# The bias of the forgetting attention as one piece for each query tile, its mask added by an accumulating DMA

## The chip, the cores and the metric

The kernel runs on one core of a Trainium2 chip. The metric is the device time of one execution in microseconds (us). The kernel before took 2027.2 us (median of three executions, 2025.74 to 2028.43).

TensorE (PE) multiplies matrices into PSUM, VectorE (DVE) and ScalarE (ACT) work on tiles in SBUF and PSUM, GpSimd (POOL) works on tiles in SBUF and issues accumulating DMAs, and SyncE (SP) issues plain DMAs. Each engine takes its instructions in a fixed order and stands still while the next one waits.

## The reference, cut to what matters

A block of three transformer layers on 512 tokens of width 1024. Its last two layers hold a forgetting attention (8 heads of 64) beside a retention branch. In one of these layers, for the attention alone:

```
log_f  = log_sigmoid(f_logit + b_forget)            # 512 x 8
c      = cumsum(log_f over tokens)                  # one row of 512 numbers per head
scores = (q_i @ k.T) * 64 ** -0.5                   # 128 queries of block i x 512 keys
bias   = c_i[:, None] - c[None, :]
logits = where(key <= query, scores + bias, -inf)
out_i  = softmax(logits) @ v
```

In a softmax over keys `c_i` drops out (it is the same along a row), so a head needs the row of `c` over the keys, the same for every query, and the causal mask, which matters only in the 128x128 square on the diagonal.

## The kernel before, in words

The 512 tokens are four tiles of 128. Each weight block of 512 KB is loaded by SyncE into one of three `wr` buffers, and split into a high and a low half in float32r: ScalarE writes `wh`, VectorE writes `wl` (`wblk`, line 351; six buffers of each). Every product is three matmuls (high by high, high by low, low by high).

`block2` (line 1261) is one of the two layers with the forgetting attention. It projects the values, then the forget gates, and writes the 8 rows of `c` to DRAM (`cd`). Then for each of four pairs of heads it projects q and k (two `proj_a` of 24 matmuls, each in one of four PSUM banks `mm`) and spawns a thread `attention_pair` (line 507). After the four pairs comes the projection of the retention values (`proj_b` with column 2568), which fills four `mm` banks at once.

`attention_pair` first makes its operands for the two heads: `qs`, `kh` and `kl` read the two `mm` banks on ScalarE and VectorE, so a bank is free again only after the second head's `qs` or `kl`. For each head it then takes the query tiles t = 3, 2, 1, 0: scores of 128(t+1) keys into an `at` bank, one or two reductions on VectorE that add the bias and keep the row's minimum (the scores carry a minus sign), an exponential on ScalarE, a reciprocal, and a scaling on VectorE. When all four tiles are done, TensorE transposes the probabilities, VectorE and ScalarE copy them out of PSUM, and TensorE multiplies with the values.

`fox_bias` (line 1193) gives the reductions their bias. Per head it loads the row of `c` into all 128 partitions (`row`, 256 KB), and GpSimd adds the constant `tri` (0 on and below the diagonal, 1e30 above it, repeated for each tile) into a second tile `cm`. Tile t then needs two reductions: the keys before the diagonal with `row`, the diagonal square with `cm` (tile 0 needs the second only). The bias of the first block's attention (`moba_bias`) is one piece for each tile already.

What sets the order: `Weave` (line 160) runs the threads against a model of each engine's cost (the classes `Weave` and `Engine`; DMAs are not in that model) and records TensorE's instructions in the order in which the model lets threads proceed. The order on the other engines is made by a scheduler when the program is built. `load` (line 345) places a plain DMA on SyncE's queue behind the newest weight load.

Of the kernel before, what the change touches and what calls it, by code (L numbers as in the profile page):

```python
# [14 lines left out]
ALU = mybir.AluOpType  # L15
# [4 lines left out]
P, T, D = 128, 512, 1024  # L20
# [133 lines left out]
class Event:  # L154


    t = None
# [110 lines left out]
def model_kernel(ctx: ExitStack, tc: tile.TileContext, I, out):  # L268
    nc = tc.nc
# [13 lines left out]
    act, dve, pool = Engine(nc.scalar, wv, 0.2, 0.83), Engine(nc.vector, wv, 0.17, 1.04), Engine(nc.gpsimd, wv, 0.25, 2.1)  # L283
    uid = [0]

    def nm(s):
        uid[0] += 1
        return f"{s}_{uid[0]}"

    def bt(s="b", dt=F32):  # L290
        return pb.tile([P, T], dt, tag="b", name=nm(s))
# [31 lines left out]
    def copy(o, i):  # L323
        act.activation(o, i, AF.Copy)
# [20 lines left out]
    def load(dst, src):  # L345

        with tc.issue_after(last_dma[0].ins):
            nc.sync.dma_start(dst, src)

    def wblk(*key, pieces=1):  # L350
        key = key if len(key) == 7 else (*key, "")
        off, size = offs[key]
        nk = (key[3] - key[2]) // P
        raw = pw.tile([P, 1024], F32, tag="wr", name=nm("wr"), bufs=3)
        src = I["wall"][off : off + size].rearrange("(p w) -> p w", p=P)
        hi = pw.tile([P, 1024], F32R, tag="wh", name=nm("wh"))
        cuts = [slice(1024 // pieces * i, 1024 // pieces * (i + 1)) for i in range(pieces)]
        for c in cuts:
            with tc.issue_after(xdma[0].ins) if xdma else nullcontext():
                last_dma[0] = nc.sync.dma_start(raw[:, c], src[:, c])  # L360
            copy(hi[:, c], raw[:, c])
        if key[6]:
            h3 = hi.rearrange("p (k w) -> p k w", k=nk)
            r3 = raw.rearrange("p (k w) -> p k w", k=nk)
            sub_lo(h3[:, :, 32:64], r3[:, :, 32:64], h3[:, :, 32:64])
            return h3
        lo = pw.tile([P, 1024], F32R, tag="wl", name=nm("wl"))
        for c in cuts:
            sub_lo(lo[:, c], raw[:, c], hi[:, c])
        return hi.rearrange("p (k w) -> p k w", k=nk), lo.rearrange("p (k w) -> p k w", k=nk)  # L370
# [48 lines left out]
    def proj_b(name, l, k0, k1, c, acts, done, koff=0, tail=0, wait_k=False, wait_t=False, pre=None):  # L419


        pss = [mm_ps() for _ in range(NT)]
        ks = list(range(k0 // P, k1 // P))
        steps = [ks[i : i + 2] for i in range(0, len(ks) - tail, 2)] + ([ks[len(ks) - tail :]] if tail else [])
        for st in steps:
            if pre is not None:
                pre(st[0])
            pieces = 2 if pre is not None and st[0] == 0 else 1
            ws = [wblk(name, l, k * P, (k + 2) * P, c, c + 512, pieces=pieces) for k in st[::2]]
            if pre is not None:  # L430
                pre(st[1])
            if wait_k:
                for k in st:
                    yield acts.ev[k - koff]
            for t in range(NT):
                if wait_t:
                    yield acts.ev[t]
                last = st[-1] == ks[-1]
                yield from form_b(pss[t], ws, acts, [k - koff for k in st], t, st[0] == ks[0], last)
                if last:  # L440
                    done(t, pss[t])


    def const_src(n):
        return I["c128"][:, slice(*_AT[n])]

    def const(n):
        src = const_src(n)
        t = bt(n)[:, 0 : src.shape[1]]
        load(t, src)  # L450
        return t
# [4 lines left out]
    def col(n, i=0):  # L456
        return cols[:, _COL[n][0] + i : _COL[n][0] + i + 1]
# [42 lines left out]
    def row_bcast(src, n0):  # L500

        t = bt("row")
        load(t, bass.AP(tensor=src.tensor, offset=src.offset + n0, ap=[[0, P], [1, T]]))
        return t
# [97 lines left out]
    def token_rows(src, t, n):  # L602
        return src[t * P : t * P + P, 512 * n : 512 * n + 512]
# [334 lines left out]
    def to_tokens(dst, scaled):  # L938
        def done(t, ps):
            v = bt("v")  # L940
            if scaled:
                act.activation(v, ps, AF.Identity, scale=r1[:, t : t + 1])
            else:
                copy(v, ps)
            dst.append(v)

        return done

    def low_proj(w, n, acts):

        ps = mm_ps()
        for k in range(8):
            mm(ps, w[:, k, :], acts.hs[k], k == 0, False)
            mm(ps, w[:, k, :], acts.ls[k], False, k == 7)
            yield 0
        f = bt("low")
        copy(f[0:n], ps[32 : 32 + n])
        dve.tensor_tensor(f[0:n], ps[0:n], f[0:n], ALU.add)
        return f
# [230 lines left out]
        yield from block2(0, xw2, h)  # L1190


    def fox_bias(cd, tri):
        def bias(h):
            cb, cm = row_bcast(cd, T * h), bt("cm")
            pool.tensor_tensor(cm, cb, tri, ALU.add)

            def pieces(t):
                d = (P * t, P * t + P, cm[:, P * t : P * t + P])
                return [d] if t == 0 else [(0, P * t, cb[:, 0 : P * t]), d]  # L1200

            return pieces

        return bias

# [55 lines left out]
    def block2(l, xw, h):  # L1261
        fv = []
        yield from proj_b("w_in_2", l, 0, D, 1024, xw, to_tokens(fv, False), tail=8, wait_t=True)
        f = yield from low_proj(wblk("w_in_2", l, 0, D, 1536, 1544, "low"), 8, xw)
        a = bt("fa")
        dve.tensor_scalar(f[0:8], f[0:8], col(f"bf{l}")[0:8], None, ALU.add)
        log_sigmoid(f[0:8], f[0:8], a[0:8])
        dve.tensor_tensor_scan(a[0:8], one[0:8].to_broadcast([8, T]), f[0:8], 0.0, ALU.mult, ALU.add)
        cd = pd.tile([8, T], F32, tag="cd", name=nm("cd"))
        nc.sync.dma_start(cd, a[0:8])  # L1270
        bias = fox_bias(cd, const("tri"))
        mix = Acts(8, "mix")
        for i in range(4):
            qk = []
            for j in range(2):
                qk.append((yield from proj_a("w_in_2", l, 512 * j + P * i, xw)))

            def operands(q, k):
                def get():
                    return q, k, -0.125, None  # L1280
                    yield

                return get

            wv.spawn(attention_pair(i, operands(*qk), fv, bias, mix), 1)
        vs = []
        yield from proj_b("w_in_2", l, 0, D, 2568, xw, to_tokens(vs, False))
        ccos, csin = const("cc"), const("ss")
        decay, xi, zeta = const("decay"), const("xi"), const("zeta")
        sgs = []  # L1290
        for i in range(4):
            qk = []
            for j in range(2):
                ps = yield from proj_a("w_in_2", l, 1544 + 512 * j + P * i, xw)
                a, b = bt("ra"), bt("rb")
                copy(b[0:64], ps[64:128])
                copy(b[64:128], ps[0:64])
                dve.tensor_tensor(a, ps, ccos, ALU.mult)
                pool.tensor_tensor(b, b, csin, ALU.mult)
                pool.tensor_tensor(a, a, b, ALU.add)  # L1300
                qk.append(a)
            sgs.append([Event(), bt("sg")])
            wv.spawn(ret_head(l, i, *qk, vs, decay, xi, zeta, sgs[i], mix), 1)
        for i in range(4):
            ps = yield from proj_a("w_in_2", l, 3080 + P * i, xw)
            ev, sg = sgs[i]
            sigmoid(sg, ps)
            dve.tensor_tensor(sg, ps, sg, ALU.mult)
            wv.mark(ev)
        hT = Acts(8, "hT", True)  # L1310
        ln1 = LayerNorm(h, norm_rows("ln1_g_2", "ln1_b_2", l))

        def norm1(t):
            ln1.apply(t)
            yield from to_features(h[t], hT, t)

        yield from out_proj("w_out_2", l, mix, h, ALPHA, ln1.part, norm1)
        ln2 = LayerNorm(h, norm_rows("ln2_g_2", "ln2_b_2", l))
        if l == 0:
            xw2 = Acts(8, "xT", True)  # L1320

        def norm2(t):
            ln2.apply(t)
            if l == 0:
                yield from to_features(h[t], xw2, t)
            else:
                for n in range(2):
                    nc.sync.dma_start(token_rows(out, t, n), h[t][n])

        yield from ffn("w_ff1_2", "w_ff2_2", l, hT, h, ALPHA, ln2.part, norm2, 6)  # L1330
        if l == 0:
            yield from block2(1, xw2, h)
# [45 lines left out]
```

## Time and profile before

| | |
|---|---|
| median of three executions | 2027.2 us |
| the profiled execution | 2023.48 us, its span 2021.7 us |
| TensorE busy | 1986.7 us, 98% of the span |
| VectorE busy | 1165.7 us, 58% |
| ScalarE busy | 936.4 us, 46% |
| GpSimd busy | 281.8 us, 14% |
| DMA | 240.50 MB, mean 119 GB/s |

How to read it: a group of instructions is named by line, engine, operation and tiles (output <- inputs, buffer numbers left out). Line 311 is every matmul, line 320 every transpose, line 262 every instruction on VectorE, ScalarE and GpSimd, line 348 every plain load other than weights. Of the tiles, `mm` and `at` are PSUM banks, `ea`, `eb`, `ec` the scores and probabilities of a head (tile 3 in `ea`, tile 2 and tile 0 in `eb`, tile 1 in `ec`), `mx` their small columns. The two layers with the forgetting attention have theirs at about 860 to 955 us and 1456 to 1552 us.

### The profile page before, as it was taken

The page shows a single profiled execution, that of the slowest core. Times are in us where ns is not written, and L with a number is a line of the kernel's source. Part 1 is how long each engine was busy: PE and PEld are TensorE (multiplying, and loading weights), DVE is VectorE, ACT ScalarE, POOL GpSimd, SP SyncE. Part 2 cuts the span into 40 slices and gives each one's busy share as a digit, 9 for nine tenths or more (in the row PEclk, how much of TensorE's full clock was granted, in tenths as well). Part 3 has the DMA queues.
Part 4 walks back from the last instruction along what each step waited for, and adds up shares of the span by engine and source line. Part 5 has one row for each costly group of instructions (what it writes and reads, how often), then busy time and mean ns, then how long its engine had stood idle before and what let it go on. Part 6 is the DMA issues. An engine that isn't in the chain of part 4 may idle for free.

```text
span 2021.7 us, 25560 instructions
## 1 busy us (share of the span) xinstructions
PE 1986.7 (98%) x9574; PEld 1646.3 (81%) x9574; DVE 1165.7 (58%) x2052; ACT 936.4 (46%) x1639; POOL 281.8 (14%) x313
## 2 busy tenths in 40 slices
PE   8999999999999999999999999999999999999998
PEld 7777788888888888877888888888877889888886
DVE  6676444444556573475455656665575565656655
ACT  6566354333545453365332554552464324545550
POOL 2000110000212110010401201110111401211101
PEclk9999999999999999999999999999999999999999
DMA  6422123242766543332233745552422234655551
GB/s 202 157 90 78 53 65 103 94 146 74 187 162 133 155 125 115 100 106 88 78 126 111 158 138 134 148 148 81 132 94 84 73 115 146 135 156 156 131 142 42
DMA packets 93483, 240.50 MB, mean 119 GB/s; under 512 B 10734, under 2 KB 11200, under 8 KB 93360
## 3 DMA queue, kind: packets, MB, share of 16 engines
q1 hardware_dynamic: 72624, 201.12, 29.6%
q0 software_dynamic: 20736, 37.76, 11.5%
q8 instruction: 75, 1.23, 0.2%
q14 instruction: 48, 0.39, 0.1%
HBM read 236.69 MB, written 4.77 MB: 119 GB/s over the span
## 4 chain that ended last, share of the span: by engine, by line
PE 95%; DVE 2%; ACT 2%; issue 0%; POOL 0%; DMA 0%; POOLq 0%; DVEq 0%; SPq 0%; ACTq 0%
PE mm L311 67%; PE at L311 26%; PE at L320 2%; ACT wh L262 0%; DVE wl L262 0%; ACT kh L262 0%; ACT qs L262 0%; DVE og L262 0%; DVE h L262 0%; DVE qs L262 0%; POOL mv L262 0%; POOL gm L262 0%; ACT kl L262 0%; DMA xr<-in_xT_dram 0%; DVE cum L262 0%
## 5 line engine op out<-in xcount | busy, mean ns | idle before, releaser
L262 DVE TENSOR_TENSOR wl<-wr,wh 128x1024 fp32r<-128x1024 f32 (+1 forms) x265 | 334.9, 1266 | 316.7 <-ACT wh L262 315.1
L262 ACT ACTIVATE wh<-wr 128x1024 fp32r<-128x1024 f32 (+1 forms) x268 | 283.1, 1057 | 486.0 <-PE mm L311 346.4
L262 DVE TENSOR_TENSOR wl<-sw,wh 128x512 fp32r<-128x512 f32 x252 | 167.2, 688 | 179.1 <-ACT wh L262 178.9
L262 ACT ACTIVATE wh<-sw 128x512 fp32r<-128x512 f32 x252 | 151.2, 626 | 229.5 <-PE at L311 124.0
L311 PE MATMUL at<-hTh,wl 128*128 128x512 f32 (+1 forms) x640 | 242.2, 378 | 0.0
L311 PE MATMUL at<-hTh,wh 128*128 128x512 f32 (+1 forms) x640 | 242.2, 378 | 0.0
L311 PE MATMUL at<-hTl,wh 128*128 128x512 f32 (+1 forms) x640 | 242.2, 378 | 0.0
L311 PE MATMUL mm<-xTh,wh 128*128 128x512 f32 x536 | 213.9, 399 | 0.0
L669 POOL DMA_DIRECT2D sw<-in_wall_dram x144 | 126.6, 1016 | 600.2 <-DVE wl L262 504.6
L311 PE MATMUL mm<-xTl,wh 128*128 128x512 f32 x536 | 209.0, 390 | 0.0
L311 PE MATMUL mm<-xTh,wl 128*128 128x512 f32 x512 | 200.0, 391 | 0.0
L311 PE MATMUL mm<-wh,xl 128*128 128x512 f32 x504 | 196.1, 389 | 0.0
L311 PE MATMUL mm<-wl,xh 128*128 128x512 f32 x504 | 196.1, 389 | 0.0
L311 PE MATMUL mm<-wh,xh 128*128 128x512 f32 x504 | 196.1, 389 | 0.0
L311 PE MATMUL mm<-wh,xTh 128*128 128x512 f32 x352 | 144.5, 411 | 12.8 <-ACT wh L262 6.6
L311 PE MATMUL mm<-wl,xTh 128*128 128x512 f32 x352 | 139.0, 395 | 0.0
L311 PE MATMUL mm<-wh,xTl 128*128 128x512 f32 x352 | 138.9, 395 | 0.0
L311 PEld LDWEIGHTS at<-hTh,wl 128*128 128x128 f32 x640 | 120.4, 188 | 22.5
L311 PEld LDWEIGHTS at<-hTl,wh 128*128 128x128 f32 x640 | 120.4, 188 | 22.4
L311 PEld LDWEIGHTS at<-hTh,wh 128*128 128x128 f32 x640 | 120.4, 188 | 22.4
L311 PEld LDWEIGHTS mm<-xTh,wh 128*128 128x128 f32 x536 | 100.8, 188 | 19.6 <-ACT wh L262 0.5
L311 PEld LDWEIGHTS mm<-xTl,wh 128*128 128x128 f32 x536 | 100.9, 188 | 18.7
(283 smaller groups left out, 3705.1 us busy)
## 6 DMA issues: line engine op xcount, KB each, us to landing
wr<-in_wall_dram SPq DMA_DIRECT2D x266, 512.0 KB, 3.6
sw<-in_wall_dram SPq DMA_DIRECT2D x144, 256.0 KB, 5.7
sw<-in_wall_dram POOLq DMA_DIRECT2D x144, 256.0 KB, 6.0
row<-cd SPq DMA_DIRECT2D x16, 256.0 KB, 4.1
revp<-rev SPq DMA_DIRECT2D x1, 2560.0 KB
xr<-in_xT_dram SPq DMA_DIRECT2D x8, 256.0 KB, 6.1
g<-revp SPq DMA_DIRECT2D x8, 256.0 KB, 4.1
h<-in_x_dram SPq DMA_DIRECT2D x8, 256.0 KB, 5.7
```

What stands on the lines that cost most here:

```text
L262: return f(out, *a, **k)
L311: nc.tensor.matmul(out, lhsT, rhs, start=start, stop=stop, skip_group_check=more)
L320: nc.tensor.transpose(out, in_, ident)
L669: nc.gpsimd.dma_start(t, src, accum_op=ALU.add)
```

## The change

Each query tile gets a bias tile of its own: for each head and each t, SyncE loads 128(t+1) entries of the row of `c` into all partitions (`c1`, `c2`, `c3` hold tiles 1; 2 and 0; 3), and an accumulating DMA on GpSimd's queue adds the 128x128 mask from DRAM to the last 128 columns. GpSimd's addition, the constant tile `tri` and its load are gone, and every tile has one reduction.

```diff
-    def fox_bias(cd, tri):
+    def fox_bias(cd):
+        room = [None]
         def bias(h):
-            cb, cm = row_bcast(cd, T * h), bt("cm")
-            pool.tensor_tensor(cm, cb, tri, ALU.add)
-
-            def pieces(t):
-                d = (P * t, P * t + P, cm[:, P * t : P * t + P])
-                return [d] if t == 0 else [(0, P * t, cb[:, 0 : P * t]), d]
-
-            return pieces
+            if h % 2 == 0:
+                room[0] = bt("c1")
+            a, b, c = bt("c3"), bt("c2"), room[0]
+            h0 = 256 * (h % 2)
+            tiles = [b[:, 384:512], c[:, h0 : h0 + 256], b[:, 0:384], a]
+            for t in (3, 2, 1, 0):
+                n = P * t + P
+                load(tiles[t], bass.AP(tensor=cd.tensor, offset=cd.offset + T * h, ap=[[0, P], [1, n]]))
+                nc.gpsimd.dma_start(tiles[t][:, P * t : n], const_src("tri")[:, 0:P], accum_op=ALU.add)
+            return lambda t: [(0, P * t + P, tiles[t])]
...
-        bias = fox_bias(cd, const("tri"))
+        bias = fox_bias(cd)
```

The new form moves instructions on every engine, in the same way in both layers. The first place is SyncE's queue at the first pair of heads, where `wr` is a weight block and `row` or `c` the bias; before:

```order
L1270 DMA cd_6799<-fa_6792 8x512 [waits DVE_49]
L360 DMA wr_7458<-in_wall_dram 128x1024 [waits DMAHW3_49,DVE_49]
L348 DMA row_6900<-cd_6799 128x512 [waits DMAHW7_49,PE_49]
L360 DMA wr_7575<-in_wall_dram 128x1024 [waits DMAHW4_49,DVE_49]
L348 DMA row_6913<-cd_6799 128x512 [waits PE_49]
```

and now:

```order
L1276 DMA cd_6799<-fa_6792 8x512 [waits DVE_49]
L360 DMA wr_7577<-in_wall_dram 128x1024 [waits DMAHW3_49,DVE_49]
L348 DMA c_1264_6899<-cd_6799 128x512 [waits DMAHW6_49,PE_49]
L348 DMA c_1265_6900<-cd_6799 128x384 [waits PE_49]
L348 DMA c_1263_6898<-cd_6799 128x256 [waits DMASW1_49,PE_49]
L348 DMA c_1265_6900<-cd_6799 128x128
L348 DMA c_1263_6898<-cd_6799 128x256 [waits DMAHW4_49]
L348 DMA c_1269_6918<-cd_6799 128x512 [waits DMAHW5_49,PE_49]
L348 DMA c_1270_6919<-cd_6799 128x384 [waits DMASW2_49]
L348 DMA c_1270_6919<-cd_6799 128x128 [waits DMAHW7_49]
L360 DMA wr_7656<-in_wall_dram 128x1024 [waits DMAHW0_49,DVE_49]
```

Eight loads for two heads stand in a row, and the next weight load behind them. GpSimd issues the eight masks in the same order of tiles.

The second place is TensorE from the last matmul of the fourth pair's k projection (`mm_7250` before, `mm_7358` now) to the first matmul of the retention values that wants the bank of the fourth pair's q. Before (rows that repeat are left out):

```order
L311 MATMUL mm_7250<-xTh_3889,wl_7255 128x512
L311 MATMUL mm_7364<-wh_7369,xTh_3888 128x512
...
L320 MATMUL at_7377<-ident,eb_7066 128x128 [waits DVE_49,PE_49]
...
L311 MATMUL mm_7365<-wh_7369,xTh_3888 128x512
...
L320 MATMUL at_7419<-ident,ec_7063 128x128 [waits DVE_49,PE_49]
...
L311 MATMUL mm_7366<-wh_7369,xTh_3888 128x512 [waits DVE_49]
```

and now:

```order
L311 MATMUL mm_7358<-xTh_3889,wl_7363 128x512
L311 MATMUL mm_7438<-wh_7443,xTh_3888 128x512
...
L311 MATMUL at_7451<-pta_7274,v_6687 64x512 [waits Activation_49]
...
L311 MATMUL at_7462<-kh_7297,qs_7296 128x512 [waits DVE_49]
...
L320 MATMUL at_7541<-ident,eb_7318 128x128 [waits DVE_49]
...
L311 MATMUL mm_7439<-wh_7443,xTh_3888 128x512
...
L311 MATMUL mm_7440<-wh_7443,xTh_3888 128x512 [waits DVE_49]
```

Before, 12 matmuls of the projections and 8 transposes stand between the two; now 12 matmuls, the second pair's product with the values (`at_7451`), the eight score matmuls of the third pair's second head (from `at_7462`) and 4 transposes.

The third place is VectorE at the same point, up to the second `qs` of the fourth pair, which frees that bank. Before:

```order
L262 TENSOR_TENSOR wl_7840<-wr_7836,wh_7837 128x1024 [waits DMAHW0_49,PE_49,Activation_49]
L262 RECIPROCAL mx_7340<-mx_7340 128x1 [waits Activation_49]
L262 COPY pta_7326<-at_7377 128x512 [waits PE_49]
L262 TENSOR_SCALAR eb_7194<-eb_7194,mx_7340 128x384 [waits DVE_49]
L262 SCALAR_TENSOR_TENSOR qs_7383<-mm_7155,qs_7383 64x512 [waits Activation_49]
L262 TENSOR_TENSOR kl_7385<-mm_7250,kh_7384 64x512 [waits Activation_49]
L262 SCALAR_TENSOR_TENSOR qs_7396<-mm_7155,qs_7396 64x512 [waits Activation_49]
```

and now:

```order
L262 TENSOR_TENSOR wl_7866<-wr_7862,wh_7863 128x1024 [waits DMAHW3_49,PE_49,Activation_49]
L262 TENSOR_TENSOR mixl_6810<-at_7451,mixh_6802 128x512 [waits Activation_49]
L262 ISA ea_7433,mx_7465<-at_7462,c_1360_7305 128x512 [waits DMAHW2_49,DMASW5_49,PE_49]
...
L262 ISA eb_7434,mx_7488<-at_7478,c_1361_7306 128x128 [waits DMASW7_49]
...
L262 SCALAR_TENSOR_TENSOR qs_7495<-mm_7249,qs_7495 64x512 [waits Activation_49]
...
L262 TENSOR_SCALAR ea_7433<-ea_7433,mx_7465 128x512 [waits DVE_49]
...
L262 TENSOR_SCALAR eb_7434<-eb_7434,mx_7488 128x128 [waits DVE_49]
L262 TENSOR_TENSOR kl_7497<-mm_7358,kh_7496 64x512 [waits Activation_49]
L262 SCALAR_TENSOR_TENSOR qs_7515<-mm_7249,qs_7515 64x512 [waits Activation_49]
```

The fourth pair's two `qs` now stand behind the split of the product with the values (`mixl`) and behind a whole softmax of the head before: four reductions and four scalings.

## Rows read from the trace of the kernel before

**Rows 1.** Page, chain that ended last: shares of the span by engine

```profile
PE 95%; DVE 2%; ACT 2%; issue 0%; POOL 0%; DMA 0%; POOLq 0%; DVEq 0%; SPq 0%; ACTq 0%
```

**Rows 2.** TensorE's waits, whole trace: us in total, times, longest

```profile
PE mm L311 <- DVE qs L262: 5.9, 2, 2.9
...
PE at L311 <- ACT pta L262: 1.7, 2, 0.9
```

**Rows 3.** Chain, 860 to 1120 us: start us, us, what

```profile
902.20 3.87 PE mm L311 x17
...
906.09 1.07 ACT wh L262
...
907.18 1.22 DVE wl L262
...
910.14 0.69 DVE kl L262
...
910.86 0.63 ACT kl L262
...
911.50 0.60 ACT qs L262
...
912.12 0.70 DVE qs L262
```

**Rows 4.** Windows: us, busy by engine, PEclk, DMA share, GB/s

```profile
913.00:914.00 1.00, 1.00 (x6) 0.82 (x7) 0.97 (x2) 0.66 (x2) 0.73 (x1) 1.00 0.09 33
1509.00:1511.00 2.00, 2.00 (x7) 1.51 (x6) 1.48 (x3) 0.69 (x2) 2.00 (x2) 0.54 0.00 0
1511.00:1513.00 2.00, 2.00 (x9) 1.54 (x7) 0.00 (x0) 0.00 (x0) 0.41 (x1) 0.61 0.00 0
```

**Rows 5.** VectorE groups by form, 855 to 960 us: count | busy us, mean ns | idle

```profile
L262 DVE CUSTOM_DVE_ANT_0 ea<-at,row 128x384 f32<-128x384 f32 x8 | 4.4, 551 | 0.3 <-PE at L311 0.2
L262 DVE TENSOR_SCALAR ea<-ea,mx 128x512 f32<-128x512 f32 x8 | 3.9, 482 | 0.0
...
L262 DVE CUSTOM_DVE_ANT_0 ea<-at,cm,mx 128x128 f32<-128x128 f32 x8 | 2.7, 340 | 0.1
```

**Rows 6.** The same view, 180 to 300 us

```profile
L262 DVE CUSTOM_DVE_ANT_0 ea<-at,g 128x512 f32<-128x512 f32 x2 | 1.4, 686 | 0.6 <-PE at L311 0.6
```

**Rows 7.** Timeline of SyncE's queue, 845 to 965 us: start us, us, what

```profile
858.99 0.37 SPq L348 DMA_DIRECT2D row<-cd  x1
...
876.79 0.90 SPq L348 DMA_DIRECT2D row<-cd  x2
```

**Rows 8.** Timeline of GpSimd, 840 to 965 us

```profile
862.97 1.56 POOL L262 TENSOR_TENSOR cm<-row,tri 128x512 f32<-128x512 f32 x1 [129.75 <-DMA row<-cd]
```

**Rows 9.** Timeline of VectorE, 855 to 960 us

```profile
867.60 2.34 DVE L262 TENSOR_TENSOR wl<-wr,wh 128x1024 fp32r<-128x1024 f32 x1 [0.89 <-ACT wh L262]
```

**Rows 10.** Chain again: pieces of one kind of TensorE work

```profile
869.41 1.28 PE at L311 x8
...
878.16 0.44 PE at L320 x4
```

**Rows 11.** Timeline of TensorE, 897 to 902 us

```profile
897.71 1.08 PE L311 MATMUL at<-pta,v 128*64 128x512 f32 x4
...
900.01 0.44 PE L311 MATMUL at<-kh,qs 128*128 128x384 f32 x1
```

**Rows 12.** Line 669, accumulating loads: ns min/median/max; landing min/median/max

```profile
L669 POOL DMA_DIRECT2D sw<-in_wall_dram x144: 853/872/1900, 518.9 to 1923.8; - x144
...
DMA to landing us min/median/max: 3.8/6.0/10.2
```

**Rows 13.** Timeline of GpSimd, 515 to 525 us

```profile
518.87 3.82 POOL L669 DMA_DIRECT2D sw<-in_wall_dram  x4 [28.51 <-DMA sw<-in_wall_dram]
```

**Rows 14.** DMA issues, 1100 to 1125 us: queue, count, KB each, median us to landing

```profile
sw<-in_wall_dram POOLq DMA_DIRECT2D x4, 256.0 KB, 7.3
```

**Rows 15.** Page, DMA queue: packets, MB, share of 16 engines

```profile
q0 software_dynamic: 20736, 37.76, 11.5%
```

## The prediction

> **What bounds the kernel now.** I read the page first. The chain that ended last is TensorE for 95% of the span [rows 1]; the reader is to see that time on another engine counts only where TensorE waits for it. So the second view is TensorE's waits. Two kinds belong to the forgetting attention, each twice, once in each layer: 2.9 us in which a projection matmul waits for VectorE's `qs`, and 0.9 us in which a score matmul waits for ScalarE's copy of the probabilities [rows 2]. That is 2 x 3.8 = 7.6 us of 2021.7; more the change cannot remove, apart from what the clock gives back. The third view is the chain around the 2.9 us. The fourth pair's k projection ends at 906.07 (902.20 + 3.87), then ScalarE splits a weight block, VectorE does its half, and the two heads' operands follow one another: `kl`, its copy, the second `qs` on ScalarE, the second `qs` on VectorE at 912.12 to 912.82 [rows 3]. The retention values' third bank is the one that this `qs` reads. The windows come last, for the clock: in the first layer it stays at 1.00 behind this wait, in the second it stands at 0.54 and 0.61 for four microseconds behind a wait of the same length [rows 4], which costs 2 x 0.46 + 2 x 0.39 = 1.7 us.
>
> **The change, part by part.** The sum is made against the profiled execution (2023.48 us, span 2021.7), which is 3.7 us under the median of the runs, and is then carried over to the median.
>
> TensorE has the same instructions in another order, so its own work costs nothing new.
>
> VectorE loses three reductions and three small readouts in each of 16 heads. Tile 3 had 551 + 340 ns [rows 5] and gets one of 686 [rows 6], 0.2 us less; tiles 2 and 1 save as much each, so 0.6 us a head and 10 us in all. GpSimd loses 16 additions of about 1.3 us (one of them is drawn out to 1.56 [rows 8]) and VectorE's `wl` that ran beside one took 2.34 instead of 1.22 us [rows 3, 9]. All this lies beside TensorE's work, which never waits for `cm` [rows 2], and the loads of `tri` do too: none of it is in the sum, except through the place where VectorE stands when TensorE wants it.
>
> That place is after the k projection of the fourth pair. Take the end of that projection as zero. Before, TensorE has 12 matmuls of 0.228 us (3.87 for 17 [rows 3]) and 8 transposes of 0.11 (0.44 for four [rows 10]), 3.6 us, and the second `qs` is done at 912.82 - 906.07 = 6.75: a wait of 3.1 by this count, 2.9 measured. Now TensorE has the same 12 matmuls, 2.7, the product with the values, 2.3 (897.71 to 900.01 [rows 11]), eight score matmuls, 1.28, and four transposes, 0.44 [rows 10]: 6.75 us. VectorE, by the new order, first has to split the product with the values. That product ends 0.7 + 2.3 = 3.0 after zero; ScalarE's copy (0.6, as `qs` [rows 3]) and the split (0.7, as `kl`) bring it to 4.4. Then four reductions, 1.9 less 0.2 for their overlap, to 6.1; the first `qs` to 6.8; four scalings (0.48 for the widest [rows 5], 1.2 together) and their reciprocals to 8.35; `kl`, 0.69, to 9.1; its copy, 0.63, ScalarE's second `qs`, 0.60, and VectorE's, 0.70, with the steps between them, to 11.05 [rows 3]. The wait becomes 11.05 - 6.75 = 4.3 us. It was 2.9, and the 0.9 of the score matmuls has no place in the new order (its bank is freed some 3 us early), so the layer gains nothing from the shorter reductions: 4.3 against 3.8, plus 0.5. This is the term I trust least. The end of the product with the values sets it, and VectorE's 4.4 may be off by 1 us either way: -0.5 to +1.5.
>
> The clock fell behind one wait of 2.9 us out of two. Behind two waits of 4.3 us I expect it to fall both times: 1.7 us more [rows 4]. Bounds 0 and 1.7.
>
> The bias itself now comes by a longer way. Before, `row` was issued at 858.99 [rows 7] and GpSimd could start at 862.97 [rows 8]: 4.0 us. Now eight loads leave one after the other (0.37 to 0.45 us each [rows 7], 3.3 us of SyncE's queue, with the next weight load behind them; conversions run so far ahead that the `wh` at 906.09 starts when a block six earlier is finished [rows 3], so weights do not decide). GpSimd follows with eight accumulating DMAs. Four such leave in 3.82 us [rows 13], 0.955 each. From issue to landing (call it L) those of 256 KB take 3.8, 6.0, 10.2 us at least, median and at most [rows 12]. These here have 64 KB. A packet of this queue costs 0.115 x 16 x 2021.7 / 20736 = 0.18 us of an engine [rows 15], nine packets an engine 1.6 us, of which a quarter of the bytes should save about 1.1: I take L = 5.0, between 3.8 and 6.0 and nearer the median.
>
> Two places use it. First pair: piece 7 of 8 lands at 863.0 + 6 x 0.955 + L = 868.7 + L, and VectorE ends the first head's softmax 0.75 later, 869.45 + L. TensorE starts the scores six matmuls earlier than before, 869.41 - 1.36 = 868.05, and after 21 matmuls and twice 1.28 us wants that head at 875.4 [rows 10]. It waits only if L is over 6.0. Second pair: its loads stand behind a weight load whose buffer VectorE frees after the first pair's last reduction, two scalings and a `wl` of 1.22 [rows 3]: 869.7 + L + 2.25. Then 0.4 for SyncE, 4.0 to land, five more issues (4.8) to the second head's first piece, L again, and 2.4 for a reduction, the next `wl` and two scalings that stand behind it: 883.55 + 2L. TensorE wants the first head's probabilities 72 matmuls, 32 score matmuls (5.1), 20 transposes and one product after 868.05: 894.05. At L = 5.0 half a microsecond is spare; from L = 5.25 on TensorE waits twice what L is above. At 3.8 nothing, at 6.0 1.5 us a layer. I put 0 into the sum and keep 3.0 for the range.
>
> The sum: 2 x 0.5 + 1.7 + 0 = +2.7 us, 2026.2 for the profiled execution and 2029.9 for the median.
>
> One rule speaks against this change. GpSimd's issues have a median of 0.87 us beside a busy VectorE, and one took 1.9 [rows 12]; `wl` and the addition that ran together both came out longer than alone [rows 8, 9]. The Trainium skill ("SBUF — State Buffer", SBUF: two separate sides) says that GpSimd writes the descriptors of its DMAs through a port pair that VectorE holds during its two-port operations. By that rule the scalings between the reductions would hold up the masks for the following ones; were every issue at the 1.9 of the row, the sixth piece of the second pair would come about 5 us later. The median of 0.87 shows little of it here, so the sum leaves it out and the third rival carries it.
>
> **The rivals.** (1) Faster: the four scalings do not hold up the `qs` of the fourth pair, because the product and its split come in time. Then the longer work of TensorE (6.75 against 3.6 us) covers the operands, which before were ready at 6.75; the 2.9 shrink to 0, the 0.9 is gone, the clock stays up: 2 x 3.8 + 1.7 = -9.3, 2017.9. For it speaks that VectorE has 10 us less to do; against it that the order is fixed and `qs` stands behind the softmax. Half of it, -4.6, is 2022.6. (2) Nothing: the waits change places and sum to the same, the second layer's clock falls as before: 2027. For it: the terms are small; against it, only their size. (3) Slower: the masks land late. VectorE stands at a reduction, and behind it stand `wl`, the scalings and the next pair's `qs`, for which TensorE waits. Four accumulating DMAs that were issued singly had a median of 7.3 us [rows 14]; with L = 7.3 the second pair costs 883.55 + 14.6 - 894.05 = 4.1 a layer: 2 x 4.6 + 1.7 = +10.9, 2038, and up to 2041 if the clock falls behind these waits too. It decides from L = 5.25. Against it: a quarter of the bytes, and a lighter DMA load than where the 6.0 was measured. (4) The change doesn't do what it says (a scheduler that undoes it): the order shows that it does; no chance of its own.
>
> **How the numbers follow.** Forecast 0.47, rival 1 0.15, rival 2 0.18, rival 3 0.20. The likeliest is 2029.9; its own range is 2026 to 2036 (the bounds above: -1 to +3 from the operands, 0 to 1.7 from the clock, 0 to 3 from the masks). About 0.2% (4 us) is what a measurement of this kernel can tell from no change. Faster by more than that is rival 1 alone, 0.15. Slower by more is rival 3 and the upper half of the forecast's range, some 0.2 + 0.19 = 0.39. Within: 0.46. For 8 in 10 the range takes in half of rival 1 and most of rival 3: 2021 to 2040.
>
> **What would show it right or wrong.** The profile after should show TensorE waiting for `qs` about 4 us in each layer, at the third bank of the retention values, and the clock near 0.55 behind it twice. VectorE's reductions should wait for an accumulating DMA in the first two pairs, by less than 2 us each, and 64 such DMAs should land in about 5 us. The `wl` of 2.34 us should be back at 1.22. The forecast is wrong if the wait for `qs` is under 2 us (rival 1), if TensorE waits at the transposes of the second pair (rival 3), or if weight loads arrive late.

## The result and the profile after

The changed kernel took 2050.26 us (2049.39 to 2050.52), the kernel before 2026.47 beside it: 1.0119 times as long, 95% interval 1.0106 to 1.0131, 23.8 us more. The prediction was 2029.9 with a range of 2021 to 2040: it was wrong, and wrong in size, since the slower side had 0.39.

The profiled span is 2048.5 us. On the page, the chain that ended last now has 3% of DMAs in it, where it had 0% [rows 1]:

```profile
PE 91%; DMA 3%; DVE 3%; ACT 2%; issue 1%; POOL 0%; SPq 0%; POOLq 0%; DVEq 0%; ACTq 0%
```

TensorE's waits over the whole trace (us in total, times, longest), which answer to [rows 2]:

```profile
PE at L311 <- DVE mx L262: 10.6, 5, 2.5
PE mm L311 <- DVE qs L262: 9.1, 2, 4.6
...
PE at L320 <- DVE mx L262: 2.1, 2, 1.9
PE at L320 <- DVE ptb L262: 1.1, 2, 0.5
PE at L320 <- DVE mixl L262: 0.9, 1, 0.9
```

The two `qs` waits stand where the prediction had them (4.5 and 4.6 us), and the one for `pta` is gone. New are the waits for `mx`, the rows' minima that VectorE's reductions leave: 12.7 us, of which 1.6 were there before, outside these stages. In the first layer three of them stand in TensorE's timeline (start us, us, what, in brackets the idle time before and what ended it):

```profile
876.55 0.44 PE L311 MATMUL at<-kh,qs 128*128 128x384 f32 x1 [2.05 <-DVE mx L262]
883.10 0.30 PE L320 MATMUL at<-ident,eb 128*128 128x128 f32 x1 [0.27 <-DVE mx L262]
900.35 1.08 PE L311 MATMUL at<-pta,v 128*64 128x512 f32 x4 [1.95 <-DVE mx L262]
```

and in the second layer:

```profile
1483.34 0.44 PE L311 MATMUL at<-kh,qs 128*128 128x384 f32 x1 [2.47 <-DVE mx L262]
1489.73 0.30 PE L320 MATMUL at<-ident,eb 128*128 128x128 f32 x1 [1.86 <-DVE mx L262]
1507.55 1.08 PE L311 MATMUL at<-pta,v 128*64 128x512 f32 x4 [2.52 <-DVE mx L262]
```

The windows of the first layer's attention (busy by engine, then PEclk, the granted share of TensorE's clock, DMA share, GB/s) show the second loss:

```profile
860.00:880.00 20.00, 17.95 (x79) 14.54 (x78) 8.95 (x15) 8.95 (x17) 7.03 (x8) 0.94 0.64 170
880.00:900.00 20.00, 17.58 (x85) 13.83 (x84) 12.24 (x35) 10.99 (x23) 5.87 (x7) 0.97 0.58 129
900.00:920.00 20.00, 19.65 (x100) 15.35 (x101) 15.17 (x47) 13.64 (x31) 7.99 (x10) 0.91 0.72 151
920.00:940.00 20.00, 15.53 (x78) 11.63 (x76) 12.97 (x38) 11.91 (x28) 7.33 (x9) 0.83 0.62 132
```

Before, PEclk stood at 1.00 in all of this stage. One fall to about half speed, as in [rows 4], costs 1.7 us. Here one follows the wait at 876.55, one the wait at 900.35, and two together the `qs` wait; in the second layer only the `qs` wait has a fall behind it, a double one.

I cut 840 to 980 us (first layer) and 1440 to 1600 us (second) into windows of 4 us and sum TensorE's idle time and 4 x (1 - PEclk). Before: idle 3.9 + 3.9, clock 0 + 1.7. After: idle 9.3 + 13.5, clock 6.8 + 3.4. These show where the time goes, but they overlap: at both `qs` waits the clock is already down while TensorE still stands, and 2.4 of the 10.2 us of clock lie there.

What the two stages cost is read directly. TensorE has the same 9574 records in both traces, and their order differs only from the 3994th to the 4429th and from the 6894th to the 7329th, so a record outside can be found in both. The 3901st, ahead of the first stage, is 3.3 us later than before, the 4501st, behind it, 14.0; the 6801st, ahead of the second stage, 13.9, the 7401st, behind it, 24.1. I call it the lag: 10.6 + 10.2 = 20.8 us. The medians differ by 23.8 and the profiled spans by 26.8. Of the latter 3.3 us stand ahead of the first stage, and 2.6 behind TensorE's last record, 10.6 us from there to the end instead of 8.0. Among the other kernels below the former varies from -0.2 to 5.4 and the latter from 8.0 to 10.6, so whether any of the 3 us between lag and medians belongs to the change isn't shown.

What VectorE waits for is seen in the chain of the first layer (start us, us, what):

```profile
871.60 8.44 DMA c<-in_c_dram
...
880.06 0.29 DVE eb L262
...
885.04 1.23 DVE wl L262
...
886.35 0.27 SPq L360
...
887.19 5.20 DMA c<-cd
...
892.94 7.36 DMA c<-in_c_dram
...
900.35 4.34 PE at L311 x18
```

From 871.60 to 900.35 two accumulating DMAs and a row load lead: a mask lands after 8.44 us, the first pair's reduction follows, then a `wl` that frees the buffer for a weight load, and only behind that weight load SyncE reaches the second pair's rows. 5.20 us later these are there, and their mask takes another 7.36. It is the path that the prediction drew for its third rival, up to the second pair's masks; TensorE then waits at another place than the one drawn (see below). For all 64 accumulates (the view of tile `c` on GpSimd: issue ns min/median/max; what GpSimd waited for; who waited for it; landing min/median/max):

```profile
L1207 POOL DMA_DIRECT2D c<-in_c_dram x64: 856/875/1305, 867.1 to 1544.5; - x64
...
  DMA c<-cd: 50.7, 23
...
  DVE ea L262: 10.3, 3
...
DMA to landing us min/median/max: 2.6/6.2/9.0
```

And VectorE's timeline of the first pair:

```profile
870.93 1.23 DVE L262 TENSOR_TENSOR wl<-wr,wh 128x1024 fp32r<-128x1024 f32 x1 [0.89 <-ACT wh L262]
875.79 0.69 DVE L262 CUSTOM_DVE_ANT_0 ea<-at,c 128x512 f32<-128x512 f32 x1 [3.64 <-DMA c<-in_c_dram]
```

The `wl` is back from 2.34 [rows 9] to 1.23 us, as predicted, but behind it the first reduction waits 3.64 us.

### The profile page after: what moved, and what is told of

The parts are those of the page before. It is cut to its first block, busy times and chain, and to the rows that moved or that the text cites. A ratio compares the mean times of both kernels' runs of the same rounds, so it can differ in the third digit from the quotient of the medians.

```text
span 2048.5 us, 25654 instructions
## 1 busy us (share of the span) xinstructions
PE 1995.9 (97%) x9574; PEld 1652.1 (81%) x9574; DVE 1156.9 (56%) x1956; ACT 937.2 (46%) x1639; POOL 317.0 (15%) x361
## 3 DMA queue, kind: packets, MB, share of 16 engines
q0 software_dynamic: 29952, 41.96, 13.2%
q8 instruction: 75, 1.23, 0.2%
## 4 chain that ended last, share of the span: by engine, by line
PE 91%; DMA 3%; DVE 3%; ACT 2%; issue 1%; POOL 0%; SPq 0%; POOLq 0%; DVEq 0%; ACTq 0%
PE mm L311 64%; PE at L311 25%; PE at L320 2%; DMA c<-in_c_dram 2%; DMA c<-cd 1%; DVE wl L262 0%; ACT kh L262 0%; ACT qs L262 0%; ACT wh L262 0%; DVE qs L262 0%; DMA xr<-in_xT_dram 0%; DVE eb L262 0%; ACT kl L262 0%; DVE og L262 0%; DVE h L262 0%
```

## The experiments

Theories: **A**, the masks land late (rival 3 of the prediction, at a higher price); **B**, the new order of TensorE asks too early, whatever the bias does; **C**, the many small DMAs crowd rows and weights. In the table, idle and clock are the two sums of the section above (before: 7.8 and 1.7), "lag" is what the two stages cost against before, by the same four records, "measured" the difference of the medians against before in the same set of runs, and the ratio has its 95% interval. By the names in the traces TensorE's order is that of the changed kernel in all but the four runs with the early `q`; VectorE's and ScalarE's are too in the seven runs that leave the masks out, add or copy them, take them from SBUF, or use DMAs for a part of them.

| kernel | idle, clock | lag | measured | ratio |
|---|---|---|---|---|
| changed kernel | 22.8, 10.2 | +20.8 | +23.8 | 1.0119 [1.0106, 1.0131] |
| no masks | 8.8, 5.1 | +2.6 | +1.8 | 1.0008 [0.9999, 1.0018] |
| masks by GpSimd addition | 8.9, 3.4 | +0.6 | +1.4 | 1.0007 [0.9998, 1.0017] |
| order only | 16.4, 5.1 | +10.4 | +12.1 | 1.0058 [1.0043, 1.0073] |
| order and spare DMAs | 10.4, 5.1 | +3.7 | +5.6 | 1.0027 [1.0016, 1.0038] |
| DMA masks in pair 1 | 15.8, 8.5 | +13.2 | +13.5 | 1.0065 [1.0048, 1.0082] |
| DMA masks in pairs 2 to 4 | 15.7, 5.1 | +9.6 | +8.8 | 1.0041 [1.0026, 1.0056] |
| rows accumulated | 7.7, 1.7 | -0.7 | +2.0 | 1.0009 [0.9999, 1.0019] |
| q early | 5.3, 1.7 | -3.3 | -3.3 | 0.9982 [0.9973, 0.9991] |
| one DMA mask a head | 19.8, 8.5 | +17.2 | +15.1 | 1.0077 [1.0062, 1.0092] |
| q early, old bias | 6.0, 1.7 | -3.3 | -4.0 | 0.9980 [0.9970, 0.9989] |
| q and bias early | 7.3, 3.4 | +0.4 | +0.6 | 1.0005 [0.9996, 1.0015] |
| three loads | 7.2, 1.7 | -1.0 | +0.1 | 1.0004 [0.9995, 1.0014] |
| plain copies | 21.1, 10.2 | +20.3 | +20.2 | 1.0099 [1.0084, 1.0114] |
| mask from SBUF | 20.4, 8.6 | +17.6 | +20.2 | 1.0101 [1.0084, 1.0118] |

The lag of the one profiled execution comes within 3 us of every measured difference. The runs one by one:

**No masks.**

```diff
-                nc.gpsimd.dma_start(tiles[t][:, P * t : n], const_src("tri")[:, 0:P], accum_op=ALU.add)
```

> The changed kernel without its 64 accumulating DMAs: the causal mask is left out, the 64 row loads, the one reduction for each tile and TensorE's order stay as they are. Theory A (the accumulating DMAs land late, and nothing else): the 12.7 us in which TensorE waited for mx go to under 2 us, the 9.1 us for qs stay, the clock falls at most behind qs: 2028 to 2033 us. Theory B (TensorE's new order asks for the scores and probabilities too early, whatever the bias does): the mx waits stay, 2044 us or more. Theory C (the many small DMAs crowd each other and the weights): the row loads still land in about 7 us, half of the loss stays, 2036 to 2043 us.

2027.44 us. A holds, a little better than its range; B and C fall. The row loads land late here too (medians of 6.1 to 8.4 us by size in the first layer, 6.1 to 9.2 in the changed kernel) and TensorE hardly pays for it.

**Masks by GpSimd addition.**

```diff
-                nc.gpsimd.dma_start(tiles[t][:, P * t : n], const_src("tri")[:, 0:P], accum_op=ALU.add)
+                nc.gpsimd.tensor_tensor(tiles[t][:, P * t : n], tiles[t][:, P * t : n], tri[:, 0:P], ALU.add)
```

> The changed kernel with each accumulating DMA replaced by an addition of tri on GpSimd, on the same 128 columns of the same tile. TensorE's order is the same. Theory A: the addition ends some 0.5 us after its load instead of 6.2, the mx waits are under 3 us, 2028 to 2034 us. Theory B: 2044 us or more. Theory C: the row loads land as late as before, 2038 to 2045 us, and VectorE waits for GpSimd, which waits for the loads.

2027.01 us: A again, 1 us under its range. Of the 23.8 us, 22.4 go with the accumulating DMAs. TensorE's waits here:

```profile
PE mm L311 <- DVE qs L262: 8.5, 2, 4.3
...
PE at L311 <- DVE mx L262: 1.6, 1, 1.6
```

The `qs` waits (4.3 and 4.2) are the predicted term; the `mx` wait is the old one outside these stages.

**Order only.** The bias is that of before; the planner is charged as in the change:

```diff
-            pool.tensor_tensor(cm, cb, tri, ALU.add)
+            nc.gpsimd.tensor_tensor(cm, cb, tri, ALU.add)
...
+                wv.charge(dve, 0.17 + 1.04 * n / 1000.0, (e[:, 0:n], s[:, 0:n]))
                 for j, (a, b, tl) in enumerate(pieces(t)):
-                    dve.tensor_tensor_reduce(...)
+                    nc.vector.tensor_tensor_reduce(...)
```

> The kernel before (row and cm, two reductions for tiles 3, 2 and 1) with only the planner's charges of the change: TensorE's instructions stand in exactly the order of the changed kernel. Theory A: the order alone costs little; the qs wait grows from 2.9 to between 4.3 and 5.5 us a layer, no mx wait over 1 us, 2028 to 2033 us. Theory B: the order is the loss, 2044 us or more. Theory C: as A.

2037.70 us, between A and B: a miss. TensorE's waits:

```profile
PE mm L311 <- DVE qs L262: 9.0, 2, 4.5
PE at L320 <- DVE ptb L262: 6.7, 2, 3.4
```

The `qs` wait is as expected; the 3.4 us a layer for `ptb`, a copy on VectorE, are not. With the old bias the new order costs 12.1 us, with the new one, without DMA masks, 1.4. B holds for this pairing alone, and the next run shows that it isn't the second reduction by itself.

**Order and spare DMAs.** The run before, plus a `spare` after each pair that issues the change's loads and accumulates into tiles `x1`, `x2`, `x3`, which nothing reads.

> The same as the order-only kernel, and after the bias of each pair the changed kernel's eight row loads and eight accumulating DMAs as well, into tiles that nothing reads. Theory A: nobody waits for them, so within 3 us of the order-only kernel. Theory B: as the order-only kernel. Theory C: the traffic itself delays rows and weights, 8 us or more above the order-only kernel, with TensorE or ScalarE waiting for wr.

2031.27 us, 6.4 under the order-only kernel, which no theory foresaw. VectorE's and ScalarE's orders came out otherwise here (by the names in the traces at least 12 and 4 instructions stand elsewhere), and the `ptb` waits fell from 6.7 to 2.4 us: the two kernels differ in more than traffic. What it does show: with the 64 row loads and the 64 accumulates under way beside it, a kernel with the same order of TensorE and the same two reductions loses 5.6 us and not 23.8. C falls, though its own rows land in 7.3 us instead of 3.9 (first layer, medians).

**DMA masks in pair 1, and in pairs 2 to 4.** The kernel with GpSimd additions, with

```diff
+                if h < 2:      # the other run: h >= 2
+                    nc.gpsimd.dma_start(tiles[t][:, P * t : n], const_src("tri")[:, 0:P], accum_op=ALU.add)
+                else:
                     nc.gpsimd.tensor_tensor(...)
```

> The kernel with GpSimd additions (2027.0 us), but with accumulating DMAs for the first pair of heads of each layer: 16 of 64. TensorE and VectorE keep their order. Theory A1 (each pair pays for its own late masks): the mx wait of the first pair comes back, 2.0 to 2.5 us a layer, and a little clock: 2031 to 2036 us. Theory A2 (only the first pair is late by itself, and the lateness is handed on through the weight load that stands behind it): nearly the whole loss, 2042 us or more.

2039.64 us, above the range of A1 and below that of A2: against before 12.1 more than with additions alone (13.5 and 1.4).

> The opposite of the run before: GpSimd additions for the first pair, accumulating DMAs for the other three, 48 of 64. A1: the waits at the second and third pair come back, 2.5 to 5 us a layer, and the clock falls behind them: 2035 to 2044 us. A2: 2026 to 2031 us.

2034.91 us: 7.4 more, at the lower edge of A1's range (2035). Together 19.5 of the 22.4 us, so nearly additive. A quarter of the masks makes more than half of the loss. A reason, not tested by itself, is that the first pair's rows can't be asked for before `cd` is written. The lateness is not handed on there: all new waits of the pair-1 run stand at the first pair itself, for `mx` 1.9 and 0.8 us in the first layer and 3.2 in the second, for `ptb` 0.5 in each. The sum of the clock is 5.1 us higher than with additions.

**Rows accumulated.** Masks and zeros one pair ahead, then one DMA behind `cd`:

```diff
+                    load(tiles[t][:, P * t : P * t + P], const_src("tri")[:, 0:P])
+                    if t:
+                        nc.gpsimd.memset(tiles[t][:, 0 : P * t], 0.0)
...
+                nc.gpsimd.dma_start(tiles[t], row, accum_op=ALU.add)
```

> The two DMAs of each tile in the opposite order: the mask is loaded onto the diagonal square and zeros are set beside it one pair ahead, and the row of cd is then accumulated by the GpSimd queue over the whole width. Still 64 accumulating DMAs (256, 192, 128 and 64 KB), but behind cd only one DMA stands in series instead of two. Theory A3 (the series of two landings is the loss): 2027 to 2034 us. Theory A4 (the rate at which GpSimd's queue issues and lands accumulates is the loss): 2042 us or more, since they carry more bytes.

2028.20 us: A3. The same count of accumulating DMAs, with four times the bytes in the largest, and landings no shorter (256 KB 7.2, 192 KB 7.8 us), costs 2.0 us against before instead of 23.8. With additions, too, only one landing stands behind `cd`: what the change lost, it lost by putting two in series. (The 2.0 is no clean price of the accumulates: the rows no longer stand behind a weight load on SyncE, and two instructions of VectorE and ten of ScalarE stand elsewhere.)

**q early.** From the kernel with additions (`split_q`, not shown, does what `attention_pair` did with q):

```diff
                 ps = yield from proj_a("w_in_2", l, 512 * j + P * i, xw)
+                if j == 0:
+                    wv.fork()
+                    ps = [split_q(ps, -0.125, hh) for hh in range(2)]
                 qk.append(ps)
```

> The kernel with GpSimd additions for all masks, and the q operand of each pair split as soon as q's own projection is done, 5.5 us before k's, so that its bank does not wait behind k and the softmax of the pair before. Theory: the qs wait of 4.2 us a layer goes to under 1.5 us and with it 1 to 1.7 us of clock: 2017 to 2023 us. Rival: the wait goes to kl at the fourth bank, 2024 to 2028 us.

2022.85 us, inside the range. The `qs` waits of both layers are gone; what TensorE waits for instead:

```profile
PE at L311 <- DVE mixl L262: 3.6, 2, 1.8
...
PE at L320 <- DVE eb L262: 1.7, 2, 0.9
```

**One DMA mask a head.** Additions for tiles 2, 1, 0, the accumulating DMA for t == 3:

> GpSimd additions for tiles 2, 1 and 0, an accumulating DMA for tile 3 alone: 16 of 64, spread over all pairs, the mask that is wanted first. Theory A5 (an accumulate takes 6 us and more by itself): the landing keeps a median of 5.5 us or more, TensorE waits for mx again in the first pair, 2031 to 2039 us. Theory A6 (the eight accumulates and eight loads of a pair crowd each other, and one alone would land in about 4 us): a median of 4.5 us or less, 2026 to 2030 us.

2041.17 us, 13.7 more than with additions alone (15.1 and 1.4). The landing keeps a median of 6.6 us (2.8 to 9.6): A5, though the price is above its range. So 16 accumulates land no earlier than 64, but the 64 row loads are still beside them in this run. In the chain of the first layer a row load and its mask follow one another directly:

```profile
859.92 4.11 DMA c<-cd
864.03 9.62 DMA c<-in_c_dram
```

**q early, old bias.** The kernel before with that edit alone.

> The kernel before, with its bias in two pieces, and only the early split of q. If the gain of the run with the early q (2022.9 us) is the early q alone: 2019 to 2024 us. If it needs the one reduction for each tile too: 2025 to 2036 us, with TensorE waiting for ptb as in the order-only run.

2022.07 us, the fastest of all, and it owes nothing to the change: ratio 0.9980 [0.9970, 0.9989]. It beats both kernels; the `q` early on top of additions is as fast within its interval.

**q and bias early; three loads.**

```diff
+                    ready = {2 * i + hh: bias(2 * i + hh) for hh in range(2)}
...
-            wv.spawn(attention_pair(i, operands(*qk), fv, bias, mix), 1)
+            wv.spawn(attention_pair(i, operands(*qk), fv, ready.get, mix), 1)
```

> The kernel with the early q and GpSimd additions, and the row loads and additions of a pair issued at q too, 5.5 us earlier. TensorE's order stays. If a late bias still holds anything up: 2018 to 2021.5 us. If it doesn't (no mx wait in the two attention stages of the run with the early q): within 1.5 us of 2022.9.

2026.66 us: a miss, 3.9 slower against before than the run with the early q. The `mixl` wait went from 1.8 to 2.7 us a layer and the clock lost 1.7 more. VectorE's order differs between the two (by the names in the traces at least 32 instructions stand elsewhere); which of them does it stays open.

> As the run with q and bias early, with three row loads a head instead of four (512, 384 and 256 columns; tile 0 is added from the 256 ones): SyncE is held 4.5 instead of 6 us a pair. If weights behind the row loads were late: 1 to 2 us faster than that run. If not: within 1.5 us of it.

2026.18 us, the same within its interval. Six row loads leave SyncE in 2.75 to 2.80 us where the eight of the run before took 6.0 to 6.7 (first layer), and nothing comes of it.

**Plain copies; mask from SBUF.** What makes a landing long:

```diff
-                nc.gpsimd.dma_start(tiles[t][:, P * t : n], const_src("tri")[:, 0:P], accum_op=ALU.add)
+                nc.gpsimd.dma_start(tiles[t][:, P * t : n], const_src("tri")[:, 0:P])
     # the other run:
+                nc.gpsimd.dma_start(tiles[t][:, P * t : n], tri[:, 0:P], accum_op=ALU.add)
```

> The changed kernel with its 64 DMAs on GpSimd's queue as plain copies: the same bytes, places, waits and order on every engine, but the mask overwrites the row on the diagonal square instead of being added to it (the row's part is left out there). Theory A7 (the queue and its many small pieces make it long): the landing keeps its median near 6 us, 2045 to 2052 us. Theory A8 (the accumulation does): about 4 us, 2028 to 2038 us.

2045.20 us. GpSimd's view of tile `c` here:

```profile
L1207 POOL DMA_DIRECT2D c<-in_c_dram x64: 534/544/659, 863.7 to 1540.4; - x64
...
DMA to landing us min/median/max: 2.1/5.5/8.9
```

> The changed kernel with the masks accumulated from a copy of tri that lies in SBUF instead of from HBM; the rest stands as it did. If the read from HBM is a good part of the landing: 5 us or less, 2030 to 2040 us. If it is not (A7 or A8): within 4 us of 2050.

2045.18 us, with this view:

```profile
L1207 POOL DMA_DIRECT2D c<-tri x64: 850/869/1337, 864.9 to 1538.8; - x64
...
DMA to landing us min/median/max: 2.5/5.7/8.5
```

Both give back 3.6 us of 23.8; the second, at 2045.18, falls just short of A7's lower bound (2046). Dropping the accumulation shortens the median landing by 0.7 us and the issue by 0.33, dropping the read of HBM by 0.5. A7 holds as far as it says that the accumulation is not the cause: what is left, 5.5 us, is the landing of a small DMA on GpSimd's queue in this stage. It is not this queue alone: the row loads of 64 KB on SyncE's queue, each the last of four, land in 7.6 us there (changed kernel, first layer, median). Why some take 2.1 and others 8.9 us stays open. The Trainium skill ("DMA: Bandwidth & Descriptors", Anatomy of one DMA — SWDGE (gpsimd) path) gives a DMA of this queue some 2.0 us of fixed cost plus a part by bytes; by that an estimate for 64 KB is 2.15 us. The shortest landings here (2.1 to 2.6) agree with it, the medians of 5.5 to 6.2 do not, so here the figure is a floor and not what the stage gives.

## Why the prediction was wrong, step by step

**What failed: L.** "A packet of this queue costs ... of which a quarter of the bytes should save about 1.1: I take L = 5.0." 64 KB landed in 6.2 us in the median, and 256 KB weights in the same trace in 6.0: the bytes saved nothing. The engines' time did fall as reckoned: 17.4% of the 105 us from 855 to 960 us for 32 masks is 0.57 us of each engine for a mask, instead of 1.6, and still nine packets (4608 / 32 / 16). But that is the small part of a landing. GpSimd issued the first mask at 867.12, the first packet of its queue started at 870.70, and the reduction behind the mask at 875.79. On the path it was 8.44 and 7.36 us, and a path takes the late ones: eight masks in a row are all wanted, so a median is the wrong figure for it. The single DMAs of [rows 14] with 7.3 us were the nearer row; I had given them to a rival of 0.20. Two terms beside L were low as well: eight row loads held SyncE 5.7 to 6.2 us instead of 3.3, and on the path the second pair's row landed in 5.20 us instead of 4.0.

**The path held, its places only in part.** With L = 8.44 the prediction's own first condition gives a wait of 8.44 - 6.0 = 2.4 us at the transposes of the first pair's first head. TensorE stood still there for 0.3 us in the first layer and 1.9 in the second, but had already waited 2.0 and 2.5 us at the second head's scores, whose bank the late first reduction holds. For the second pair it gives 2 x (8.44 - 5.25) = 6.4 at that pair's transposes. There TensorE waited for 0.3 us at most. It waited 2.0 and 2.5 us earlier, at the first pair's product with the values, until the second pair's first reduction was done. So the sign that the prediction named for rival 3, a wait at the second pair's transposes, did not come; the prediction had left the `at` banks out. TensorE also came later than in its count, since it had lost time at the first pair.

**The price of a wait was too low.** Put into rival 3's own sum, L = 8.44 gives 2 x (0.5 + 6.4) + 1.7 = +15.5 us: 13.8 of idle time, where 15.0 was measured, and 1.7 of clock. The clock's sum rose by 8.5, from one fall to six, and 2.4 of it lies where TensorE stands anyway. Two falls are behind the first layer's waits for `mx`, and each `qs` wait has two where I had counted one.

**What held.** The `qs` wait: 4.3 predicted, 4.5 and 4.6 measured, and 4.3 and 4.2 with additions. There the clock lost 3.4 us, as counted. That the sum held too is not shown: predicted +2.7, with additions a lag of +0.6 and a median of +1.4, whose interval reaches below zero. The term that I trusted least was right, and the one put at 0 was the result. GpSimd's issues had a median of 875 ns and a maximum of 1305, and VectorE itself stood idle for the 3.64 us before the first reduction, while that reduction's mask was on its way: the stall by the shared ports that was weighed there (the Trainium skill, "SBUF — State Buffer", SBUF: two separate sides) does not show in the issues, and at the end of this landing VectorE was not running. One reading behind that rule was wrong: the addition that ran beside the `wl` of 2.34 us took 1.28, its usual length, and the one of 1.56 [rows 8] ran at another time, 4.6 us earlier. The sum doesn't use it.

**What was hidden too easily.** The shorter reductions were put at nothing, "all this lies beside TensorE's work". Under the new order it is not so: with the two pieces it cost 12.1 us in one order of VectorE and 5.6 in another, with one piece 1.4. So the pieces would cost some 4 to 11 us there, by the order they stand in. The change pays for its own order by the shorter reductions.

## What to carry to other kernels

Count the landings that stand in series behind the last thing to be computed, and price each by the slow end of its row, not by its median and not by its bytes: a DMA of 64 KB cost what one of 256 KB did. Do the part that doesn't depend on the late value first (the mask), and let one landing, or an addition (0.46 us on GpSimd here), follow it. A wait on TensorE can cost more than its length: here 15 us more of idle time came with 8.5 us more of clock, of which 6 were not hidden in a wait. And a bank that only waits for an operand already computed, as `q` here, is better freed where it was computed.

## What the runs showed of the hardware

For the same 2.10 MB in the first layer's stage (855 to 960 us), the queue line of the DMA view has 4.5 times the packets when they are accumulated; the changed kernel:

```profile
q0 software_dynamic: 4608, 2.10, 17.4%
```

and the one with plain copies:

```profile
q0 software_dynamic: 1024, 2.10, 8.1%
```

And eight row loads in a row on SyncE's queue took 5.7 to 6.2 us to issue, where single ones took 0.37 to 0.45 [rows 7] and four of GpSimd's took 3.82 [rows 13]: over both layers the first seven of the eight leave in 0.36 to 0.43 us each, and the eighth takes 2.3 to 3.0. Of six in a row, in the run with three loads, none takes over 1.01.

The first packet of GpSimd's queue comes late: 3.6 us after the first mask's issue in the changed kernel, 4.3 with plain copies (863.68 and 867.97), 3.9 from SBUF (864.93 and 868.83).
